# A two-layer attention, GLA and retention kernel: retention's gated branch goes by way of DRAM, attention's branch is projected last and by halves, attention's memory is handed on when it ends, background stages are spaced a little wider

## The chip, the cores and the metric

The kernel runs on one core of one Trainium2 chip. Its time is device microseconds from launch to end, the median of several runs; lower is better. The profile is one further execution of the same program, recorded instruction by instruction.

## The reference, cut to what matters

Two layers act on 1024 latent tokens `x` and 256 context tokens `xc`, each of 1024 columns. A layer normalizes and modulates its input, multiplies it by one wide matrix `w_in`, and splits the product into the inputs of three branches, three gates `z` (512 columns each) and three gates `g` (1024 columns each). The branches are neighbourhood attention (8 heads; each latent token sees a window of 8 x 16 latents and all the context), gated linear attention (GLA) and retention, both scanned in both directions with a state. All of them end in:

```python
def merge_branches(outs, z, g, w_branch, w_out):
    zs = jnp.split(z, N_BRANCH, axis=-1)
    gs = jnp.split(g, N_BRANCH, axis=-1)
    y = jax.nn.sigmoid(gs[0]) * ((outs[0] * jax.nn.silu(zs[0])) @ w_branch[0])
    for i in range(1, N_BRANCH):
        y = y + jax.nn.sigmoid(gs[i]) * ((outs[i] * jax.nn.silu(zs[i])) @ w_branch[i])
    return y @ w_out
```

The result is scaled by a gate from the modulation and added to the input. In layer 1 the context's own output is not needed, so queries, gates and merge run over 1024 tokens there and over 1280 in layer 0.

## The kernel before, in words

**Number format.** A dense product is three passes of TensorE: high part by high part, high by low, low by high (`mms`, line 376, is where every such matmul is recorded). So one unit of `fm` (128 output columns of `w_in` by 512 tokens) is 24 matmuls of 512 columns; the last token block of layer 0 has 256.

**Two programs interleaved by slots.** The instruction order is written out by a driver, `Drv`. `drv.gemm` is the dense stream: projections, then merge, layer by layer. Beside it run lanes and workers: `attention_lane` takes retention, GLA and neighbourhood attention one after another, and each spawns workers, one for a token chunk or for a unit of attention. In one `slot()` each worker and the dense stream are advanced twice, each lane once. The dense stream hands over after a quantum of `QUANT * drv.mult` = 3072 x `mult` matmul columns, or at the end of a unit if three quarters of that are reached (`end_unit`). So `mult` says how much dense work stands between two steps of the background. `RT_M`, `GL_M` and `NA_M1` are its values during retention, GLA (before and after attention's projections are done) and attention; it is 1.0 otherwise.

**Order of the dense stream.** Projections for retention, GLA, attention's v, then q and k; 12 groups of g gates, two units of 128 columns each and all token blocks (stored to DRAM after a tanh, line 1244); six groups of z gates in `Z_ORDER`, groups 0 and 1 for attention, 2 and 3 for GLA, 4 and 5 for retention. The evacuation of a z unit (`z_evac`, tanh at line 1259, product at 1260) loads the branch's output `o` back from DRAM (tile `ot`) and multiplies. For attention and GLA the product goes to DRAM (`b`, line 1273 and a deferred store); for retention it is split into a high and a low part in SBUF (lines 1267 to 1270). Groups 0 and 1 wait until attention has finished the first two, then all four of its head pairs (`na_out`); group 4 waits until the SBUF pool `E` exists.

**Attention** (`na`) has four pairs of heads; a pair has eight units of 128 queries, two more in layer 0 for the context. One unit is spawned every three slots. A unit loads q and its bias, computes scores, a softmax, transposes (`na_ptw`, `na_ptc`), copies them out of PSUM (`PT`, lines 992 and 995), multiplies by v (`na_o`, 1037) and copies the result (`oN`, 1040), which is stored when four units are together.

**After attention** the lane opens the pool `E` where attention's tiles were, if group 0 of z has begun (`want_E`). It then computes the modulation's gate (`mod_gate`: eight 512 KB pieces of `w_mod`, one a slot, matmuls `mod_ps` at line 210), and in layer 0 the next layer's shift and scale (`mod_ss`).

**Merge** takes the branches in the order 2, 1, 0 (retention, GLA, attention). Retention's operand is in SBUF already and a unit waits for its token block (`z_out`); the two others are loaded from DRAM and split by a worker, `load_b` (tiles `rb`, split at lines 1312 and 1313).

**Shared things.** Eight 128 x 512 buffers (`stg`) serve every evacuation and load named here: `st_g`, `st_z`, `ot`, `rb`, `gt`, `oN`. Nearly all loads and stores are issued in order by SP's queue. The `loader` lane brings half a weight group at a time: a load and a conversion (ScalarE cast at line 342, two GpSimd subtractions at line 345) need more than `LD_GAP` = 3 slots since the conversion before; a group that is needed earlier is converted on the spot (`need`).

Of the kernel before, what the change touches and what calls it, by code (L numbers as in the profile page):

```python
# [12 lines left out]
ALU = mybir.AluOpType  # L13
# [4 lines left out]
P = 128  # L18
# [12 lines left out]
NCOL = (24, 32, 32, 24)  # L31
LD_LAG, LD_GAP = 3, 3
RT_M = 1.25
GL_M = (1.1, 1.1, 1.0)
GL_N = 13
NA_M1 = 0.7
BR_ORDER = (2, 1, 0)
Z_ORDER = (2, 3, 0, 1, 4, 5)


def _next_f(c):
# [67 lines left out]
def hybrid_kernel(ctx: ExitStack, tc: tile.TileContext, A: dict, out: bass.AP):  # L109
    nc = tc.nc  # L110
    ctx.enter_context(tc.manual_schedule())
    pe, ve, sc, gp = nc.tensor, nc.vector, nc.scalar, nc.gpsimd
    drv = Drv()

    def dma(dst, src):
        nc.sync.dma_start(dst, src)
# [4 lines left out]
    def fv(ap):  # L121
        return ap.bitcast(F32)
# [26 lines left out]
    def stg(name, dt=F32):  # L149
        return pst.tile([P, 512], dt, tag="w2", name=name)  # L150
# [28 lines left out]
    def blocks(n):  # L179
        return [(t0, min(512, n - t0)) for t0 in range(0, n, 512)]  # L180
# [208 lines left out]
    def fm_unit(g, m, act, t0, nn, evac):  # L389
        ps = psg("fm")  # L390
        cs = m * P
        yield from mms(ps[:, :nn], nn,
                       ((lambda k: g.h(k, cs, P), lambda k: act.get(0, k, t0, nn)),
                        (lambda k: g.h(k, cs, P), lambda k: act.get(1, k, t0, nn)),
                        (lambda k: g.l(k, cs, P), lambda k: act.get(0, k, t0, nn))), g.kd)
        drv.evq_next.append(lambda: evac(m, t0, nn, ps[:, :nn]))
        if end_unit():
            yield
# [28 lines left out]
    L = []  # L427
    for layer in range(DEPTH):
# [6 lines left out]
        G = {}  # L435
# [12 lines left out]
        d = {"G": G, "nt": nt_out, "ntok": nt_out * P, "last": last}  # L448
# [197 lines left out]
    def gla(layer):  # L646
        d = L[layer]
        with tc.tile_pool(name=f"gla{layer}", bufs=2) as pl, tc.tile_pool(name=f"glac{layer}", bufs=1) as plc:
# [105 lines left out]

            drv.mult = GL_M[0]
            sc.preload_act_table_set("natural_log_exp_and_others")
# [130 lines left out]
    def na(layer):  # L887
        d = L[layer]
        ntok, last = d["ntok"], d["last"]
        with tc.tile_pool(name=f"na{layer}", bufs=2) as pn:  # L890
# [180 lines left out]
            for _ in range(4):  # L1071
                yield
            drv.mult = NA_M1
            for p in range(4):
# [42 lines left out]
    def projections(layer):  # L1117
        d = L[layer]
        while "h" not in d:
            yield  # L1120
        h = d["h"]
        G, nt, ntok, last = d["G"], d["nt"], d["ntok"], d["last"]
# [27 lines left out]
                    ga.done = True  # L1150
            gb.done = True

        def fm(g, ns, evac, by_block=False):
            need(g)
            units = [(m, t0, nn) for m in range(g.w // P) for t0, nn in blocks(ns[m])]
            if by_block:
                units.sort(key=lambda u: u[1])
            for m, t0, nn in units:
                yield from fm_unit(g, m, h, t0, nn, evac)
            g.done = True  # L1160

        yield from tm2(G["ret"][0], G["ret"][1], NT, spill_tm(d["ret"], 256, 256), spill_tm(d["ret"], 512, 256))
# [89 lines left out]
        def z_evac(zi):  # L1252
            def f(m, t0, nn, ps):
                r = zi * 256 + m * P
                br, ro = r // 512, r % 512
                ot = stg("ot")
                dma(ot[:, :nn], d["o"][br][ro:ro + P, t0:t0 + nn])
                st = stg("st_z")
                sc.activation(st[:, :nn], ps, AF.Tanh, scale=0.5)  # L1259
                ve.scalar_tensor_tensor(st[:, :nn], st[:, :nn], 1.0, ps, op0=ALU.add, op1=ALU.mult)  # L1260

                def w():
                    yield
                    yield
                    if br == 2:
                        bt = d["bact"][2]
                        ve.tensor_tensor(st[:, :nn], st[:, :nn], ot[:, :nn], op=ALU.mult)
                        hi, lo = bt.get(0, ro // P, t0, nn), bt.get(1, ro // P, t0, nn)
                        sc.copy(hi, st[:, :nn])
                        gp.tensor_tensor(lo, st[:, :nn], fv(hi), op=ALU.subtract)  # L1270
                        d["z_out"][t0] = d["z_out"].get(t0, 0) + 1
                    else:
                        gp.tensor_tensor(st[:, :nn], st[:, :nn], ot[:, :nn], op=ALU.mult)  # L1273
                        drv.defer(lambda: dma(d["b"][br][ro:ro + P, t0:t0 + nn], st[:, :nn]))
                drv.spawn(w())
            return f

        per_pair = 2 if last else 3
        d["z_out"] = {}
        for zi in Z_ORDER:  # L1280
            if zi < 2:
                while d.get("na_out", 0) < 2 * (zi + 1) * per_pair:
                    yield
            if zi == 0:
                d["want_E"] = True
            if zi == 4:
                while not d.get("E"):
                    yield
            yield from fm(G["z"][zi], [ntok] * 2, z_evac(zi), zi == 5)
        d["done"]["z"] = True  # L1290


    def merge(layer):
        d = L[layer]
        G, nt, ntok, last = d["G"], d["nt"], d["ntok"], d["last"]
        Ep = d["E"]
        y = Act(f"y{layer}", [U] * 5, KD, ntok, dt=F32, parts=1)
        bact = d["bact"]
        bact[1] = Act(f"bg{layer}", [U] * 5, 4, ntok)

        def load_b(br):
            pend = []
            for t0, nn in blocks(ntok) + [(None, 0)]:
                for k in range(4 if t0 is not None else 2):
                    if t0 is not None:
                        rb = stg("rb")
                        dma(rb[:, :nn], d["b"][br][k * P:(k + 1) * P, t0:t0 + nn])
                        pend.append((rb, k, t0, nn))
                    if len(pend) > 2 or t0 is None:
                        rb_, k_, u0, un = pend.pop(0)  # L1310
                        hi, lo = bact[br].get(0, k_, u0, un), bact[br].get(1, k_, u0, un)
                        sc.copy(hi, rb_[:, :un])
                        ve.tensor_tensor(lo, rb_[:, :un], fv(hi), op=ALU.subtract)
                    yield
                    yield

        def unit(g, br, bi, m, t0, nn):
            mt = m
# [32 lines left out]
            if end_unit():  # L1351
                yield

        w1 = drv.spawn(load_b(1))
        for bi, br in enumerate(BR_ORDER[:2]):
            if bi == 1:
                while not w1["done"]:
                    yield
                bact[0] = Act(f"bn{layer}", [Ep] * 5, 4, ntok)
                w1 = drv.spawn(load_b(0))  # L1360
            for mg in range(4):
                g = G["wb"][br][mg]
                need(g)
                for m in range(2):
                    for t0, nn in blocks(ntok):
                        while d["z_out"].get(t0, 0) < 4:
                            yield
                        yield from unit(g, br, bi, 2 * mg + m, t0, nn)
                g.done = True
        while not w1["done"]:  # L1370
# [2 lines left out]
        for t0, nn in blocks(ntok):  # L1373
            for m in range(8):
                g = G["wb"][0][m // 2]
# [28 lines left out]
        for gi in range(4):  # L1404
            g = G["wo"][gi]
# [8 lines left out]
    def attention_lane(layer):  # L1414
        d = L[layer]
        for key, fn in (("ret", retention), ("gla", gla), ("nqk", na)):
            while not d["done"].get(key):
                yield
            yield
            yield  # L1420
            yield from fn(layer)
        while not d.get("want_E"):
            yield
        es = d["es"] = ExitStack()
        ep = es.enter_context(tc.tile_pool(name=f"E{layer}", bufs=5))
        pgb = es.enter_context(tc.tile_pool(name=f"gb{layer}", bufs=1))
        E = (ep, "e")
        d["bact"] = {2: Act(f"br{layer}", [E] * 5, 4, d["ntok"])}
        d["E"] = E
        gate_sb = pgb.tile([98, 256], F32, tag="gate_sb", name="gate_sb")  # L1430
        d["gbc"] = [pgb.tile([P, D], F32, tag=f"gb{v}", name=f"gb{v}") for v in range(1 if d["last"] else 2)]
        with tc.tile_pool(name=f"modw{layer}", bufs=2) as pmw, tc.tile_pool(name=f"modp{layer}", bufs=1) as pm:
            yield from lane_join([drv.spawn(mod_gate(layer, pmw, gate_sb))])
            gd = dr.tile([2, D], F32, tag=f"gate_{layer}", name=f"gate_{layer}")
            for q in range(4):
                dma(gd[:, 256 * q:256 * q + 256], gate_sb[32 * q:32 * q + 2, :])
            yield
            for v, gb in enumerate(d["gbc"]):
                for q in range(2):
                    cs = slice(512 * q, 512 * q + 512)  # L1440
                    ob = stg("ob")
                    dma(ob, A["b_mod"][layer, 2048 + 512 * q:2560 + 512 * q].partition_broadcast(P))
                    dma(gb[:, cs], gd[v, cs].partition_broadcast(P))

                    def w(gb=gb, cs=cs, ob=ob):
                        for _ in range(4):
                            yield
                        gp.tensor_tensor(gb[:, cs], gb[:, cs], ob, op=ALU.add)
                    yield from lane_join([drv.spawn(w())])
            if not d["last"]:  # L1450
                yield from lane_join([drv.spawn(mod_ss(1, pm, pmw))])
        d["mod_done"] = True
# [201 lines left out]
```

## Time and profile before

| | us |
|---|---|
| median of 3 runs | 2956.39 (2952.46 to 2957.08) |
| profiled execution | 2953.91 |
| its span, first to last instruction | 2952.1 |
| TensorE matmul busy | 2828.3 (96%) |
| VectorE, ScalarE, GpSimd busy | 1499.4, 1102.1, 1078.2 |
| DMA | 418.69 MB, mean 142 GB/s |

Matmuls are pipelined, so a TensorE that is busy need not be at its peak. The idle time in front of an instruction matters only on the engine that bounds the stage. A group's line number can be that of a helper (376 for every dense matmul), so groups are told apart by tile names: `fm` is a projection by features, `tm` one by tokens, `mg` a merge product.

### The profile page before, as it was taken

Reading aid. Unit: us, or ns where it says so; the run is one execution under the profiler, and the core shown is the slowest. Engines: PE = TensorE matmul, PEld = TensorE weight load, DVE = VectorE, ACT = ScalarE, POOL = GpSimd, SP = SyncE. Lnnn points to the kernel's source line nnn. Section 1 sums busy time; section 2 is a strip of 40 time slices with the busy share of each in tenths; the row PEclk is TensorE's granted clock in tenths of the full one; section 3 lists DMA queues with packets and bytes.
Section 4 is the critical chain, followed back from the end, with each engine's and each line's share of the span. In section 5 each row is a group of like instructions: output and inputs, shape, how many; then the busy total and the mean of one; then the engine's idle time right before and its main releaser. Section 6 shows DMA issues by size and latency. Waiting matters only on the chain. (4 is left out here: it accounts for less than half of the span.)

```text
span 2952.1 us, 51923 instructions
## 1 busy us (share of the span) xinstructions
PE 2828.3 (96%) x19776; PEld 2433.6 (82%) x19776; DVE 1499.4 (51%) x3189; ACT 1102.1 (37%) x2569; POOL 1078.2 (37%) x1010
## 2 busy tenths in 40 slices
PE   7999999999999998899999999999999999879999
PEld 5999987788878887677899999987788788767889
DVE  5156567767514455424334346469766156562331
ACT  4133556554423434322113323456544244342110
POOL 4222125466411122043655332125665212204463
PEclk8999999999999999999999999999999999999999
DMA  6344433443244556467445354443433455645543
GB/s 239 107 142 130 139 105 111 115 133 104 92 144 135 170 151 189 125 199 233 136 126 149 104 166 119 132 121 109 145 111 111 148 160 182 181 125 164 183 129 108
DMA packets 390857, 418.69 MB, mean 142 GB/s; under 512 B 33788, under 2 KB 310284, under 8 KB 390608
## 3 DMA queue, kind: packets, MB, share of 16 engines
q1 hardware_dynamic: 353248, 361.59, 40.9%
q10 hardware_dynamic: 37360, 53.79, 5.2%
q8 instruction: 156, 2.56, 0.4%
q14 instruction: 93, 0.76, 0.1%
HBM read 302.72 MB, written 112.54 MB: 141 GB/s over the span
## 5 line engine op out<-in xcount | busy, mean ns | idle before, releaser
L376 PE MATMUL fm<-h,whi 128*128 128x512 f32 (+1 forms) x3936 | 922.6, 380 | 7.7 <-ACT st_g L1244 7.7
L345 POOL TENSOR_TENSOR wlo<-wraw,whi 128x512 fp32r<-128x512 f32 (+1 forms) x336 | 450.5, 1362 | 1000.4 <-ACT whi L342 892.0
L376 PEld LDWEIGHTS fm<-h,whi 128*128 128x128 f32 x3936 | 681.1, 190 | 157.8 <-issue 26.4
L376 PE MATMUL fm<-h,wlo 128*128 128x512 f32 (+1 forms) x1968 | 470.6, 374 | 0.0
L376 PEld LDWEIGHTS fm<-h,wlo 128*128 128x128 f32 x1968 | 339.8, 189 | 70.8 <-issue 8.7
L376 PE MATMUL tm<-whi,h 128*128 128x256 f32 (+1 forms) x2528 | 339.2, 284 | 2.0 <-ACT h L295 2.0
L376 PEld LDWEIGHTS tm<-whi,h 128*128 128x128 f32 x2528 | 318.2, 189 | 3.5 <-ACT h L295 2.7
L342 ACT CAST whi<-wraw 128x1024 fp32r<-128x1024 f32 (+1 forms) x168 | 175.8, 1048 | 268.4 <-PE tm L376 123.8
L376 PE MATMUL tm<-wlo,h 128*128 128x256 f32 (+1 forms) x1264 | 189.7, 286 | 0.0
L376 PEld LDWEIGHTS tm<-wlo,h 128*128 128x128 f32 x1264 | 166.6, 189 | 0.7 <-issue 0.2
L843 DVE TENSOR_TENSOR ek<-dd,kd 128x512 f32<-128x512 f32 x108 | 101.2, 937 | 93.4 <-ACT dd L833 93.2
L376 PE MATMUL tm<-whi,yy 128*128 128x256 f32 x1152 | 147.4, 280 | 0.0
L376 PEld LDWEIGHTS tm<-whi,yy 128*128 128x128 f32 x1152 | 140.7, 188 | 0.1
L1273 POOL TENSOR_TENSOR st_z<-st_z,ot 128x512 f32<-128x512 f32 (+1 forms) x40 | 48.2, 1209 | 253.1 <-DMA ot<-o 103.7
L798 POOL TENSOR_TENSOR dd<-Ac,ash 128x256 f32<-128x256 f32 x126 | 116.3, 923 | 51.5 <-ACT ash L785 31.0
L1260 DVE SCALAR_TENSOR_TENSOR st_z<-st_z,fm 128x512 f32<-128x512 f32 (+1 forms) x60 | 37.8, 633 | 174.4 <-ACT st_z L1259 172.5
L844 DVE SCALAR_TENSOR_TENSOR eq<-dd,g_col,qd 128x256 f32<-128x256 f32 x126 | 117.5, 933 | 13.1 <-ACT dd L833 13.0
L1244 ACT ACTIVATE st_g<-fm 128x512 f32<-128x512 f32 (+1 forms) x120 | 66.5, 557 | 144.0 <-PE fm L376 95.7
L1392 DVE TENSOR_TENSOR st_o<-tm,gb 128x256 f32<-128x256 f32 x72 | 30.5, 424 | 155.1 <-PE tm L376 152.0
L1334 DVE SCALAR_TENSOR_TENSOR gt<-gt,mg 128x512 f32<-128x512 f32 (+1 forms) x80 | 50.7, 634 | 112.5 <-PE mg L376 98.7
L833 ACT ACTIVATE dd<-dd 128x512 f32<-128x512 f32 x126 | 79.4, 635 | 75.3 <-POOL dd L799 73.1
L416 DVE COPY st_tm<-tm 128x256 f32<-128x256 f32 (+1 forms) x59 | 25.2, 428 | 161.5 <-PE tm L376 161.1
(1573 smaller groups left out, 4757.8 us busy)
## 6 DMA issues: line engine op xcount, KB each, us to landing
wraw<-in_w_in SPq DMA_DIRECT2D x104, 512.0 KB
wt<-in_w_mod SPq DMA_DIRECT2D x48, 512.0 KB
gd<-st_g ACTq DMA_DIRECT2D x96, 256.0 KB
gt<-gd SPq DMA_DIRECT2D x96, 256.0 KB
bt<-in_na_bm SPq DMA_DIRECT2D x32, 384.0 KB
ot<-o SPq DMA_DIRECT2D x48, 256.0 KB
wraw<-in_w_branch SPq DMA_DIRECT2D x24, 512.0 KB
v<-ret SPq DMA_DIRECT2D x38, 256.0 KB
```

The costliest lines, as they stand in the source:

```text
L342: sc.copy(hi[:, :, :w], raw[:, :, :w])
L345: gp.tensor_tensor(lo[:, ks, :w], raw[:, ks, :w], fv(hi[:, ks, :w]), op=ALU.subtract)
L376: pe.matmul(ps, a(k), b(k), start=i == 0, stop=i == tot - 1)
L798: gp.tensor_tensor(dv[:, :, Lh:], av[:, :, Lh:], rv, op=ALU.subtract)
L833: sc.activation(E_, E_, AF.Exp)
L843: ve.tensor_tensor(ek_, E_, kd_, op=ALU.mult)
L844: ve.scalar_tensor_tensor(eq[:, :, Lh:], ev[:, :, Lh:], rsc, qv[:, :, Lh:], op0=ALU.mult, op1=ALU.mult)
L1244: sc.activation(st[:, :nn], ps, AF.Tanh, scale=0.5)
L1260: ve.scalar_tensor_tensor(st[:, :nn], st[:, :nn], 1.0, ps, op0=ALU.add, op1=ALU.mult)
L1273: gp.tensor_tensor(st[:, :nn], st[:, :nn], ot[:, :nn], op=ALU.mult)
L1334: ve.scalar_tensor_tensor(gt[:, :nn], gt[:, :nn], 1.0, ps[:, :nn], op0=ALU.add, op1=ALU.mult)
L1392: ve.tensor_tensor(st[:, :256], ps, gbc[0 if t < LT else 1][:, 256 * gi:256 * gi + 256], op=ALU.mult)
```

## The change

Z groups 2 to 5 come first and 0 and 1 last; a wait can now be given for each half (128 columns) of a group, so each half of groups 0 and 1 waits for one more pair of attention's heads. All z products go to DRAM, retention's too. The pool `E` is opened as soon as attention's lane ends. `load_b` becomes a function of its own and also loads retention's branch, started by the lane after attention and once group 5's stores have had six slots; for that branch it takes one step of a worker for each piece, not two. Merge waits for it as a whole. `GL_M[2]` goes from 1.0 to 1.1, `NA_M1` from 0.7 to 0.8.

```diff
-GL_M = (1.1, 1.1, 1.0)
+GL_M = (1.1, 1.1, 1.1)
-NA_M1 = 0.7
+NA_M1 = 0.8
-Z_ORDER = (2, 3, 0, 1, 4, 5)
+Z_ORDER = (2, 3, 4, 5, 0, 1)
...
-        def fm(g, ns, evac, by_block=False):
+        def fm(g, ns, evac, wait=None):
             need(g)
-            units = [(m, t0, nn) for m in range(g.w // P) for t0, nn in blocks(ns[m])]
-            if by_block:
-                units.sort(key=lambda u: u[1])
-            for m, t0, nn in units:
-                yield from fm_unit(g, m, h, t0, nn, evac)
+            for m in range(g.w // P):
+                while wait is not None and not wait(m):
+                    yield
+                for t0, nn in blocks(ns[m]):
+                    yield from fm_unit(g, m, h, t0, nn, evac)
             g.done = True
...
-                    if br == 2:
-                        bt = d["bact"][2]
-                        ve.tensor_tensor(st[:, :nn], st[:, :nn], ot[:, :nn], op=ALU.mult)
-                        hi, lo = bt.get(0, ro // P, t0, nn), bt.get(1, ro // P, t0, nn)
-                        sc.copy(hi, st[:, :nn])
-                        gp.tensor_tensor(lo, st[:, :nn], fv(hi), op=ALU.subtract)
-                        d["z_out"][t0] = d["z_out"].get(t0, 0) + 1
-                    else:
-                        gp.tensor_tensor(st[:, :nn], st[:, :nn], ot[:, :nn], op=ALU.mult)
-                        drv.defer(lambda: dma(d["b"][br][ro:ro + P, t0:t0 + nn], st[:, :nn]))
+                    gp.tensor_tensor(st[:, :nn], st[:, :nn], ot[:, :nn], op=ALU.mult)
+                    drv.defer(lambda: dma(d["b"][br][ro:ro + P, t0:t0 + nn], st[:, :nn]))
...
         for zi in Z_ORDER:
+            wait = None
             if zi < 2:
-                while d.get("na_out", 0) < 2 * (zi + 1) * per_pair:
-                    yield
-            if zi == 0:
-                d["want_E"] = True
-            if zi == 4:
-                while not d.get("E"):
-                    yield
-            yield from fm(G["z"][zi], [ntok] * 2, z_evac(zi), zi == 5)
+                def wait(m, zi=zi):
+                    return d.get("na_out", 0) >= (2 * zi + m + 1) * per_pair
+            yield from fm(G["z"][zi], [ntok] * 2, z_evac(zi), wait)
+            if zi == 5:
+                def stored():
+                    for _ in range(12):
+                        yield
+                    d["want_b2"] = True
+                drv.spawn(stored())
...
+    def load_b(layer, br):
+        d = L[layer]
+        bact, ntok = d["bact"], d["ntok"]
...
                     yield
-                    yield
+                if br < 2:
+                    yield
...
-        w1 = drv.spawn(load_b(1))
+        while not d.get("b2") or not d["b2"]["done"]:
+            yield
+        w1 = drv.spawn(load_b(layer, 1))
...
-                        while d["z_out"].get(t0, 0) < 4:
-                            yield
...
-        while not d.get("want_E"):
-            yield
         es = d["es"] = ExitStack()
...
         d["E"] = E
+        while not d.get("want_b2"):
+            yield
+        d["b2"] = drv.spawn(load_b(layer, 2))
```

## Rows read from the trace of the kernel before

**Rows 1.** The page, part 1: an engine's busy time, share, instructions.
```profile
PE 2828.3 (96%) x19776; PEld 2433.6 (82%) x19776; DVE 1499.4 (51%) x3189; ACT 1102.1 (37%) x2569; POOL 1078.2 (37%) x1010
```
**Rows 2.** Waits of TensorE over the span: us in total, times, longest.
```profile
PE na_o L1037 <- DVE PT L992: 35.0, 19, 10.1
```
**Rows 3.** Sums by stage: busy us and instructions of each engine, clock, DMA, GB/s.
```profile
1158.60:1222.60 64.00, 44.76 (x363) 36.41 (x361) 44.31 (x151) 32.87 (x113) 7.07 (x6) 0.91 0.42 123
...
2347.00:2564.10 217.10, 217.10 (x1390) 179.92 (x1390) 126.50 (x350) 88.97 (x265) 45.56 (x35) 1.00 0.57 173
2564.10:2643.20 79.10, 53.23 (x442) 43.95 (x440) 52.37 (x175) 36.65 (x126) 6.54 (x5) 0.89 0.46 134
...
1325.00:1360.00 35.00, 35.00 (x217) 25.42 (x217) 18.05 (x37) 9.84 (x16) 9.27 (x8) 1.00 0.91 305
...
1232.00:1262.00 30.00, 30.00 (x184) 22.06 (x183) 5.28 (x10) 4.10 (x7) 6.02 (x6) 1.00 0.61 179
```
**Rows 4.** Chain of waits, layer 1: start us, length us, what.
```profile
2203.40 1.08 PE gla_lv L813 x32
...
2232.50 1.08 PE gla_lv L813 x32
...
2404.94 1.24 PE na_o L1037 x20
...
2435.72 1.25 PE na_o L1037 x20
...
2652.70 0.54 PE mod_ps L210 x8
...
2674.41 46.08 PE fm L376 x198
```
**Rows 5.** Sums by stage of line 1040 alone: ScalarE's busy us and instructions.
```profile
1158.60:1222.60 64.00, 2.93 (x11) 0.91 0.42 123
...
2564.10:2643.20 79.10, 2.93 (x11) 0.89 0.46 134
```
**Rows 6.** The page, part 5: count, busy us, mean ns, idle before.
```profile
L1273 POOL TENSOR_TENSOR st_z<-st_z,ot 128x512 f32<-128x512 f32 (+1 forms) x40 | 48.2, 1209 | 253.1 <-DMA ot<-o 103.7
...
L1260 DVE SCALAR_TENSOR_TENSOR st_z<-st_z,fm 128x512 f32<-128x512 f32 (+1 forms) x60 | 37.8, 633 | 174.4 <-ACT st_z L1259 172.5
```
**Rows 7.** Line 1244 in each layer: ns min/median/max, first to last start in us.
```profile
L1244 ACT ACTIVATE st_g<-fm x72: 364/592/619, 592.6 to 1039.6; 128x512 f32<-128x512 f32 x48, 128x256 f32<-128x256 f32 x24
...
L1244 ACT ACTIVATE st_g<-fm x48: 577/598/647, 2112.3 to 2464.3; 128x512 f32<-128x512 f32 x48
```
**Rows 8.** Timeline of SP's queue where attention's first loads are issued.
```profile
821.12 1.11 SPq L116 DMA_DIRECT2D k<-nkh  x2
...
2302.78 1.13 SPq L116 DMA_DIRECT2D k<-nkh  x2
```
**Rows 9.** Waits of TensorE from 593 to 840 and from 2105 to 2300.
```profile
PE gla_lv L813 <- DVE eq L845: 4.7, 4, 1.4
...
PE gla_lv L813 <- DVE eq L845: 3.6, 1, 3.6
```
**Rows 10.** Timeline of ScalarE, line 342, in layer 1's GLA stage.
```profile
2207.09 1.06 ACT L342 CAST whi<-wraw 128x1024 fp32r<-128x1024 f32 x1
...
2236.20 1.06 ACT L342 CAST whi<-wraw 128x1024 fp32r<-128x1024 f32 x1
```
**Rows 11.** Timeline of TensorE at three points; idle time before it in brackets.
```profile
1161.33 0.93 PE L1037 MATMUL na_o<-PT,vcx 128*64 128x128 f32 x8 [2.14 <-ACT PT L995]
...
2575.45 1.79 PE L1037 MATMUL na_o<-PT,vw 96*64 96x128 f32 x11 [10.06 <-DVE PT L992]
...
2647.56 0.75 PE L210 MATMUL mod_ps<-wt,csi 128*2 128x256 f32 x8 [2.72 <-DMA wt<-in_w_mod]
```
**Rows 12.** Timeline of ScalarE, layer 1, late in attention; idle before in brackets.
```profile
2573.61 0.60 ACT L1259 ACTIVATE st_z<-fm 128x512 f32<-128x512 f32 x1 [6.03 <-DMA b<-st_z]
```
**Rows 13.** DMA from 1325 to 1360, rate in 40 equal slices.
```profile
GB/s 389 293 173 384 375 377 187 288 349 358 222 367 373 310 355 411 386 377 215 276 361 358 225 332 376 321 345 342 324 373 392 231 37 194 251 73 164 306 369 377
```

More of the change, by code (lines that the diff above doesn't have):

```diff
@@ L1278, in projections @@
         per_pair = 2 if last else 3
-        d["z_out"] = {}
         for zi in Z_ORDER:
+            wait = None
             if zi < 2:
-                while d.get("na_out", 0) < 2 * (zi + 1) * per_pair:
-                    yield
-            if zi == 0:
-                d["want_E"] = True
-            if zi == 4:
-                while not d.get("E"):
-                    yield
-            yield from fm(G["z"][zi], [ntok] * 2, z_evac(zi), zi == 5)
-        d["done"]["z"] = True
+                def wait(m, zi=zi):
[7 more added lines that the diff above has]
+                drv.spawn(stored())
+        d["done"]["z"] = True
+    def load_b(layer, br):
+        d = L[layer]
+        bact, ntok = d["bact"], d["ntok"]
+        pend = []
+        for t0, nn in blocks(ntok) + [(None, 0)]:
+            for k in range(4 if t0 is not None else 2):
+                if t0 is not None:
+                    rb = stg("rb")
+                    dma(rb[:, :nn], d["b"][br][k * P:(k + 1) * P, t0:t0 + nn])
+                    pend.append((rb, k, t0, nn))
+                if len(pend) > 2 or t0 is None:
+                    rb_, k_, u0, un = pend.pop(0)
+                    hi, lo = bact[br].get(0, k_, u0, un), bact[br].get(1, k_, u0, un)
+                    sc.copy(hi, rb_[:, :un])
+                    ve.tensor_tensor(lo, rb_[:, :un], fv(hi), op=ALU.subtract)
+                yield
+                if br < 2:
+                    yield
     def merge(layer):
@@ L1299, in merge @@
         bact[1] = Act(f"bg{layer}", [U] * 5, 4, ntok)
[L1301 to L1313, printed above, removed]
-                    yield
-                    yield
         def unit(g, br, bi, m, t0, nn):
@@ L1359, in merge @@
                 bact[0] = Act(f"bn{layer}", [Ep] * 5, 4, ntok)
-                w1 = drv.spawn(load_b(0))
+                w1 = drv.spawn(load_b(layer, 0))
             for mg in range(4):
```

## The prediction

> **What bounds the kernel now.** I read the engine sums first, then the waits of TensorE, then the sums by stage, and last the chain of waits for the beat inside each stage. TensorE is busy for 96% of the span [rows 1], so a change pays only where TensorE stands idle or runs at half clock. Its longest waits in total are for VectorE's copy of the transposed probabilities, an instruction of neighbourhood attention [rows 2]. They lie in one place in each layer. Both stages called "starved" below begin when the projections have run out of work that is allowed and attention still has units to do: 1158.6 to 1222.6 in layer 0 and 2564.1 to 2643.2 in layer 1. There TensorE is busy for 44.76 of 64.0 us and 53.23 of 79.1 us, at a mean granted clock of 0.91 and 0.89, while the filled stage before (2347 to 2564.1) has it busy throughout at 1.00 [rows 3].
>
> The projections run dry because z0 waits for attention's first two pairs, z1 for all four, and z4 and z5 stand behind z1. After attention there are therefore z1, z4 and z5 still to do, with nothing beside them.
>
> **The beat.** Dense projection: 198 matmuls in 46.08 us, 0.2327 us for one of 512 columns. Filled attention: from 2404.94 to 2435.72 are three units, 10.26 us each. A unit is three slots, thus six quanta; at 0.7 a group of 24 matmuls is cut 5, 5, 5, 5, 4, so a unit brings 28.8 matmuls, 6.70 us. That leaves 3.56 us of TensorE for attention itself [rows 4]. Each starved stage shows 11 output copies [rows 5], a unit in 5.8 and 7.2 us: 11 x 3.56 = 39.2 us of real work, so 24.8 us are lost in layer 0 and 39.9 us in layer 1.
>
> **Part 1: z4 and z5 ahead of z0, and z0, z1 by halves.** Work is not changed, only its place. What it adds under attention, counted in 512-column matmuls: two groups (240 in layer 0, 192 in layer 1) and the first half of z1, which now needs only the third pair (60 and 48). Z4 and z5 bring their evacuations into the filled stage: a tanh, a VectorE and a GpSimd pass, one load and one store on SP's queue for each of 12 (8) units. In the filled stage VectorE is busy 126.5, ScalarE 89.0 and GpSimd 45.6 of 217.1 us [rows 3], so I cost the passes at nothing; without that cover VectorE's and GpSimd's are 0.63 and 1.21 us for a unit [rows 6], 15 us over eight of them. SP's two issues are weighed under part 5.
>
> **Part 2: GLA's multiplier 1.0 to 1.1** takes back part of this supply. It acts from the end of the attention projections to the end of GLA: 592.6 [rows 7] to 821.1 and 2112.3 to 2302.8 [rows 8]. Eight slots take 29.10 us there (2203.40 to 2232.50) [rows 4], 3.64 each, so these are 63 and 52 slots. The quantum grows from 3072 to 3379 columns, but matmuls are whole: in layer 1 two units of 24 are cut in seven pieces where there were eight, 12 to 13.71 a slot; in layer 0 a 512, 512, 256 triple is cut in nine where there were ten, 12 to 13.33. That is 84 and 89 matmuls more done beside GLA, which ends some 20 us later, with TensorE full in both cases. What it can win is the waits for VectorE in that stretch, 4.7 and 3.6 us [rows 9]; I take 2, bounds 0 and 8.3. What it can cost: the loader lane converts a half group at most every fourth slot; two ScalarE casts stand 29.1 us apart, with one between them [rows 10], exactly eight slots for a group. A group of layer 1 now lasts seven slots, so about every fourth group a half must be converted on the spot: two times a 1.05 us cast, 2 us; bounds 0 and 8 (every one of 52/7 groups).
>
> **Part 3: attention's multiplier 0.7 to 0.8.** With units of 512 columns five matmuls pass either threshold (2150 and 2458 columns), and the last four end the unit at 0.7 and at 0.8. Layer 1 is not changed at all. In layer 0 the 256-column units change the mean from 28.8 to 30 matmuls a unit: 28 units eat 34 more.
>
> **Part 4: the sum of the supply.** Layer 0: 240 + 60 - 84 - 34 = 182, at 30 a unit 6.1 of the 11 starved units are filled. Layer 1: 192 + 48 - 89 = 151, at 28.8 a unit 5.2 units. In shares of the lost time: layer 0 24.8 x 6.1/11 = 13.8 us. In layer 1 one wait of 10.06 us at the start of the starved stage is set aside: ScalarE stood 6.03 us for a store of a z product to land before it could reuse the buffer, and the probabilities queued behind it [rows 11, 12]. The rest gives (39.9 - 10.1) x 5.2/11 = 14.1 us.
>
> **Part 5: that hitch.** It comes when units shorten from 10.3 to 5.8 us and SP's queue, with its z loads and stores among attention's loads, falls behind. The same moment in layer 0 shows 2.14 us [rows 11]. One start with it and one without: I take half back, 5 us, bounds 10 saved and 10 more lost (a second one in layer 0).
>
> **Part 6: the way into the merge.** Retention's product now goes out to DRAM and comes back once attention has ended, because its tile lies in attention's memory. The store hides in the filled stage. The load can't: from attention's end to the first merge matmul stand only the last half of z1 and the gate's modulation matmuls. Bytes before that point: layer 0 twelve pieces 2.6 MB, eight modulation weights 4.2 MB, z1's loads and stores 1.3 MB, 8.1 MB; layer 1 (eight pieces, six weights by then) 6.3 MB. Cover: 60 x 0.2327 + 8 x 0.54 = 18.3 us, and 48 x 0.2327 + 6 x 0.54 = 14.4 us [rows 4]. TensorE's instructions stand in one written order, so a late modulation weight holds up z1 behind it: it waited 2.72 us for the first one already [rows 11]. SP's order is the same: each weight is issued behind one or two pieces, and a piece that has no free buffer holds the weights. The trace has no such stretch, so from both sides: at the 305 GB/s of 1325 to 1360, where weights, pieces and gates ran together and TensorE did not wait, 14.4 MB take 47.2 us, 14.5 over the cover; at that stretch's best slice, 411 GB/s [rows 13], 35.0, 2.3 over; at the 179 GB/s of 1232 to 1262 [rows 3] 80.4, 47.7 over. Nothing makes it a gain, as the loads are new. I take 10, near the first, whose mix of transfers it is.
> The row above shows 305 GB/s for transfers of 128 to 512 KB. The Trainium skill, "DMA: Bandwidth & Descriptors", section Bandwidth, asks for batches of 1 MiB or more and gives 341 GB/s at that size and 138 at 64 KB, which speaks against a round trip in 256 KB pieces. By 341 GB/s the 14.4 MB would cost an estimated 9.5 us over the cover, by 138 some 72; the trace's 305 lies near the first.
>
> **Sum.** 13.8 + 14.1 + 5 + 2 - 2 - 10 = 22.9 us less. The profiled execution took 2953.9 (its span is 2952.1), so 2931.0; the median of the runs is 2956.4, 2.5 us above it, and on that scale 2933.5.
>
> **Rivals.**
> *The way through DRAM decides (slower).* Place: the two entries into the merge. If the pieces and weights come at 179 GB/s because each waits for one of eight shared buffers, the entries cost 47.7 instead of 10: 22.9 - 37.7 = 14.8 us slower, 2971. It outweighs the rest from about 220 GB/s down (14.4 MB / 65.6 us, the cover plus the 32.9 us of gain). For it: the shared buffers already stop ScalarE [rows 12]. Against it: the mixed stretch at 305 with TensorE full [rows 3].
> *The widening eats the reorder (no change).* The supply goes into GLA, and both starts of starving show the 10 us wait: 13.8 + 14.1 - 10 - 14.5 - 4 = -0.6 us, thus 2957. For it: 173 of the 540 added matmuls go that way by count. Against: layer 0's start without it.
> *The fill reaches the end.* If attention needs less filler than counted, the lost time goes wholly: 64.7 + 2 - 2 - 10 = 54.7 us, 2902. Against it: the 11 units ask for 330 and 317 matmuls and get 182 and 151.
>
> **How the numbers follow.** Forecast (12 to 46 us less, 2910 to 2944) 0.72, full fill 0.05, no change 0.10, slower 0.13. The range, 2908 to 2957, takes in the no-change case and leaves out most of the full fill and of the slower case, some 0.17. A measurement of this kernel tells apart about 0.2%, 6 us. Faster than that 0.77, within it 0.10, slower 0.13.
>
> **What would show it.** Right: starved stages of some 30 us (five or six output copies without a projection between them) in each layer, eight z evacuations of layer 1 moved ahead of attention's end, only two after it; GLA ending 20 us later; merge entered 18 to 30 us earlier in total over both layers. Wrong: TensorE waiting more than 20 us for modulation weights or for retention's tile at the entries; a full-length starved stage; waits for the cast inside GLA.

## The result and the profile after

The changed kernel takes 2918.40 us in the median of 4 runs (2917.72 to 2921.78) where the kernel before took 2956.54: 38.1 us less, a ratio of 0.9876 with a 95% interval of 0.9859 to 0.9893. Forecast were 22.9 us less and 2933.5, in a range of 2908 to 2957. The profiled execution took 2921.78, the longest of its four, against 2953.91 before, so of the 38 us the two traces show 32.

On the page TensorE is busy for 7.7 us less than before [rows 1], in a span 32.1 us shorter. So 24.4 of the 32.1 us that went are idle time:

```profile
PE 2820.6 (97%) x19776; PEld 2426.7 (83%) x19776; DVE 1517.4 (52%) x3189; ACT 1099.5 (38%) x2569; POOL 1077.7 (37%) x1010
```

The waits of TensorE after (total us, times, longest). The wait for the transposed probabilities, 35.0 before [rows 2], has gone to 19.0; a wait for a weight cast of 9.8 is new:

```profile
PE mod_ps L210 <- DMA wt<-in_w_mod: 21.4, 19, 6.6
PE na_o L1037 <- DVE PT L992: 19.0, 10, 5.4
...
PE fm L376 <- ACT whi L342: 9.8, 1, 9.8
```

Sums by stage after (columns as in [rows 3]): attention without filler in layer 0, the entry into the merge, the merge; then the same for layer 1, where the first row is a stretch with filler that stops twice.

```profile
1236.20:1266.50 30.30, 20.26 (x169) 16.30 (x167) 18.51 (x62) 13.61 (x49) 1.95 (x2) 0.91 0.27 85
1266.50:1289.80 23.30, 21.33 (x122) 13.99 (x121) 8.82 (x14) 8.59 (x17) 1.29 (x1) 0.82 0.84 269
1289.80:1474.80 185.00, 182.04 (x1018) 143.79 (x1015) 80.54 (x135) 36.03 (x58) 94.39 (x75) 1.00 0.65 210
...
2577.20:2638.10 60.90, 53.92 (x345) 44.48 (x345) 36.79 (x102) 23.43 (x71) 15.66 (x13) 0.94 0.59 177
2638.10:2670.00 31.90, 24.16 (x214) 19.83 (x212) 23.13 (x76) 15.17 (x54) 1.27 (x1) 0.95 0.31 93
2670.00:2688.60 18.60, 15.72 (x81) 10.03 (x81) 5.96 (x9) 5.61 (x10) 1.67 (x1) 0.91 0.82 273
```

The 64.0 and 79.1 us without filler [rows 3] are 30.3 and 31.9 now. Line 1040, the copy of a unit's output, counts the attention units that end in them, five each where there were 11 [rows 5] (in layer 0 one copy more starts 0.1 us behind the row's edge, before and after):

```profile
1236.20:1266.50 30.30, 1.33 (x5) 0.91 0.27 85
2638.10:2670.00 31.90, 1.33 (x5) 0.95 0.31 93
```

GLA ends later, as the first load of attention shows. Line 1244 and SP's queue, the answers to [rows 7] and [rows 8]: the stretch from the first gate to attention's first load has grown from 228.5 to 243.5 us in layer 0 and from 190.5 to 212.3 in layer 1.

```profile
L1244 ACT ACTIVATE st_g<-fm x72: 377/583/643, 592.5 to 1013.4; 128x512 f32<-128x512 f32 x48, 128x256 f32<-128x256 f32 x24
...
L1244 ACT ACTIVATE st_g<-fm x48: 579/598/643, 2091.4 to 2439.3; 128x512 f32<-128x512 f32 x48
```
```profile
836.03 1.11 SPq L116 DMA_DIRECT2D k<-nkh  x2
...
2303.71 1.11 SPq L116 DMA_DIRECT2D k<-nkh  x2
```

The entry into the merge of layer 0 in TensorE's timeline (start, length, idle before in brackets): a wait of 1.97 us for the first modulation weight, and behind it twelve matmuls take 4.63 us that take 3.05 a little later. Four matmuls in front of the wait are slow too: 2.08 us, against 1.20 for the four in the last line. The mean granted clock of this stage is 0.82 (row above); the last section shows where it fell.

```profile
1266.46 2.08 PE L376 MATMUL fm<-h,whi 128*128 128x512 f32 x4
1270.50 1.03 PE L210 MATMUL mod_ps<-wt,csi 128*2 128x256 f32 x8 [1.97 <-DMA wt<-in_w_mod]
1271.46 4.63 PE L376 MATMUL fm<-h,whi 128*128 128x512 f32 x12
...
1280.09 3.05 PE L376 MATMUL fm<-h,whi 128*128 128x512 f32 x12
...
1289.79 1.20 PE L376 MATMUL mg<-br,whi 128*128 128x512 f32 x4
```

Before the change TensorE waited for the first modulation weight at the same point, when attention had ended: 2.72 us in layer 1 [rows 11], and in layer 0:

```profile
1226.61 0.61 PE L210 MATMUL mod_ps<-wt,csi 128*2 128x256 f32 x8 [1.48 <-DMA wt<-in_w_mod]
```

### The profile page after: what moved, and what is told of

Its sections match the earlier page's. It is cut to its first block, busy times and chain, and to the rows that moved or that the text cites. A ratio compares the mean times of both kernels' runs of the same rounds, so it can differ in the third digit from the quotient of the medians.

```text
span 2920.0 us, 52004 instructions
## 1 busy us (share of the span) xinstructions
PE 2820.6 (97%) x19776; PEld 2426.7 (83%) x19776; DVE 1517.4 (52%) x3189; ACT 1099.5 (38%) x2569; POOL 1077.7 (37%) x1010
## 5 line engine op out<-in xcount | busy, mean ns | idle before, releaser
L376 PEld LDWEIGHTS fm<-h,whi 128*128 128x128 f32 x3936 | 679.6, 190 | 157.2 <-issue 24.4
L1265 POOL TENSOR_TENSOR st_z<-st_z,ot 128x512 f32<-128x512 f32 (+1 forms) x60 | 73.8, 1237 | 260.7 <-DMA ot<-o 108.7
L799 POOL TENSOR_TENSOR dd<-ash,Ac 128x256 f32<-128x256 f32 x126 | 106.4, 844 | 0.0
L813 PEld LDWEIGHTS gla_lv<-eq,ek 128*64 128x64 f32 x2016 | 67.5, 139 | 42.0 <-issue 24.3
```

The costliest lines, as they stand in the source:

```text
L376: pe.matmul(ps, a(k), b(k), start=i == 0, stop=i == tot - 1)
L799: gp.tensor_tensor(dv[:, :, :Lh], rv, av[:, :, :Lh], op=ALU.subtract)
L813: pe.matmul(pl_[bk, x, h, :], ek_[:, h, bk], eq_[:, h, bk if lv else bq], start=True, stop=True)
```

## The experiments

Each ran beside the kernel before on its own chip, which takes 2952 to 2957 us from one chip to the next; I compare ratios. One per mille is 3 us. An interval reaches some 5 us to either side, so a difference between two of these kernels has to be about 7 us to be clear of the noise.

| kernel | ratio | 95% interval |
|---|---|---|
| the change | 0.9876 | 0.9859 to 0.9893 |
| multipliers alone, on the kernel before | 1.0076 | 1.0060 to 1.0091 |
| order, way and pool alone | 0.9860 | 0.9846 to 0.9875 |
| change, NA_M1 0.7 | 0.9864 | 0.9849 to 0.9879 |
| change, NA_M1 0.6 | 0.9846 | 0.9830 to 0.9863 |
| change, gate after the load | 0.9851 | 0.9836 to 0.9866 |
| change, stores a slot later | 0.9872 | 0.9855 to 0.9888 |
| change, whole groups | 0.9933 | 0.9916 to 0.9949 |
| NA_M1 0.6 and gate after the load | 0.9817 | 0.9803 to 0.9832 |
| the same with GL_M[2] 1.0 | 0.9812 | 0.9797 to 0.9826 |

**The multipliers alone.**
```diff
-GL_M = (1.1, 1.1, 1.0)
+GL_M = (1.1, 1.1, 1.1)
-NA_M1 = 0.7
+NA_M1 = 0.8
```


> The kernel before with the two multipliers alone changed (GL_M[2] 1.1, NA_M1 0.8), z order, retention's way and the pool as before. Theory A, supply: what counts is how much dense work is left when attention runs. The wider steps eat 118 matmuls in layer 0 and 89 in layer 1, so 3.9 and 3.1 more units run without filler, at some 2.6 us lost for each: 18 us slower, less about 4 us of waits saved in GLA: 2966 to 2975. Theory B, spacing: the wider steps help by themselves, because GLA's and attention's chains get more time for a step: 3 to 10 us faster, 2946 to 2953.

2977.32 us, 1.0076: slower, as supply says, by 22 us, a little more than its range. The stages without filler grow from 64.0 and 79.1 to 88.2 and 73.3 us, in layer 1 with a second stand of 20 us at 2538 outside the row:
```profile
1142.10:1230.30 88.20, 61.82 (x496) 51.10 (x495) 57.86 (x199) 40.24 (x144) 7.50 (x6) 0.90 0.37 107
2594.20:2667.50 73.30, 54.81 (x450) 45.79 (x448) 55.52 (x179) 36.61 (x126) 6.79 (x5) 0.91 0.45 131
```
Spacing as a gain in itself falls: without the reorder the wider steps are a loss.

**The rest alone** (the changed kernel).
```diff
-GL_M = (1.1, 1.1, 1.1)
+GL_M = (1.1, 1.1, 1.0)
-NA_M1 = 0.8
+NA_M1 = 0.7
```


> The changed kernel with both multipliers back (GL_M[2] 1.0, NA_M1 0.7): order, halves, DRAM way and pool alone. Theory A, supply: 118 and 89 matmuls more are there for attention, 3 to 4 units fewer without filler in each layer, 10 to 18 us, less 4 us of waits that come back in GLA: 2904 to 2912 (the changed kernel has 2918). Theory B, spacing: 5 to 15 us slower than the changed kernel, 2924 to 2933.

2913.83 us, 0.9860: the whole gain is here. Order, DRAM way and pool were not run one by one. It is 5 us better than the change by the ratios, on supply's side but short of its 2904 to 2912, and the intervals overlap. Its stages without filler are down to 4.5 and 21.8 us:
```profile
1260.00:1264.50 4.50, 2.79 (x21) 1.69 (x21) 2.44 (x4) 1.20 (x4) 3.27 (x3) 0.86 0.34 109
2637.60:2659.40 21.80, 16.55 (x138) 13.66 (x135) 16.17 (x43) 9.14 (x30) 5.25 (x4) 0.84 0.39 119
```

**NA_M1 0.7 alone.**
```diff
-NA_M1 = 0.8
+NA_M1 = 0.7
```


> The changed kernel with NA_M1 back at 0.7 alone. By the count of whole matmuls layer 1 is cut exactly as with 0.8 (pieces of 5, 5, 5, 5, 4), and layer 0 takes 28.8 instead of 30 matmuls for a unit: 34 to 40 matmuls more are left, a bit over one unit without filler less there: 2 to 4 us faster, 2914 to 2916, layer 1 the same within 1 us. Spacing: slower by 1 to 3 us.

2914.72 us, 0.9864, 3.5 us less, as counted, but within the noise. The trace is the better witness: layer 0's stage shrinks from 30.3 to 19.0 us, layer 1's stays at 31.9, since its pieces are the same.
```profile
1241.40:1260.40 19.00, 13.03 (x121) 10.32 (x121) 11.75 (x42) 8.13 (x29) 1.27 (x2) 0.97 0.23 74
2629.10:2661.00 31.90, 24.24 (x214) 19.95 (x212) 23.16 (x76) 15.18 (x54) 1.27 (x1) 0.95 0.32 93
```
This kernel and the last one differ in `GL_M[2]` alone, 1.1 here and 1.0 there. There the stages are 14.5 and 10.1 us shorter, yet the time is only about 1 us less, far within the noise. A part of it was lost again behind the stage of layer 0: TensorE waited 5.74 us for the first modulation weight there, 1.43 us here, and the way into the merge took 27.2 us there (from 1264.4 on, mean clock 0.77) and 20.9 here (from 1260.4 on, 0.95).

**NA_M1 0.6.**
```diff
-NA_M1 = 0.8
+NA_M1 = 0.6
```


> The changed kernel with NA_M1 at 0.6: a unit of 24 matmuls is cut in six pieces of four, so a unit of attention takes 24 matmuls of filler instead of 30 (layer 0) and 28.8 (layer 1). Theory A, supply: filler lasts for 5 to 8 units more, the stages without filler (30 us in layer 0, 46 in layer 1) all but vanish, 15 to 27 us less: 2891 to 2903. Theory B, spacing: at 9.1 us a unit instead of 10.3 the probabilities come late in the filled stage, TensorE waits there, 0 to 15 us more: 2918 to 2933.

2908.34 us, 0.9846, 9 us less than the change: right in direction, about half of what supply asked, though the intervals just overlap. The stage without filler is gone in layer 0 (the last 41 us of attention have TensorE busy throughout) and is 6.9 us in layer 1:
```profile
1200.00:1241.30 41.30, 41.30 (x283) 34.62 (x282) 22.97 (x57) 15.49 (x47) 11.96 (x10) 1.00 0.35 112
...
2641.40:2648.30 6.90, 4.54 (x50) 3.45 (x50) 5.48 (x10) 1.41 (x4) 3.66 (x4) 1.00 0.38 124
```
So 9.1 us for a unit is long enough for attention's chain; but a stage that vanishes gives back only what TensorE lost in it, not its length.

**Whole groups instead of halves.**
```diff
-                    return d.get("na_out", 0) >= (2 * zi + m + 1) * per_pair
+                    return d.get("na_out", 0) >= 2 * (zi + 1) * per_pair
```


> The changed kernel with the waits of z0 and z1 for whole groups again: z1 as a whole waits for all four pairs, everything else as changed. By the supply theory the halves bring 60 and 48 matmuls under attention, two units with filler in layer 0 and 1.7 in layer 1 at 2.6 to 3 us each, so without them 9 to 11 us more: 2927 to 2930; and the entry into the merge, now with four or six units of z1 to cover the modulation's weights and retention's pieces, gives 0 to 5 us of it back: 2922 to 2930. If the halves are worth nothing because the entry is only as long as its transfers, 2918.

2933.97 us, 0.9933: 17 us slower than the change, more than any case had it. The stages are 44.7 and 49.1 us:
```profile
1214.70:1259.40 44.70, 30.64 (x246) 24.87 (x243) 29.56 (x94) 21.47 (x73) 7.41 (x6) 0.90 0.35 109
2621.20:2670.30 49.10, 37.04 (x327) 30.43 (x325) 38.39 (x123) 25.26 (x85) 6.30 (x5) 0.97 0.44 134
```
So 108 matmuls, 25.1 us at 0.2327, are worth 17 us under attention by the ratios and 12 between the two profiled executions (2933.97 and 2921.78): half to two thirds of their time is free there. The prediction had 32.9 us for 333 matmuls, 77.5 us, a share of 0.42. With the noise (17 us, 7 to either side) that is not excluded.

**The gate after retention's load.**
```diff
+            yield from lane_join([d["b2"]])
             yield from lane_join([drv.spawn(mod_gate(layer, pmw, gate_sb))])
```


> The changed kernel with the modulation's gate started only when retention's branch is loaded: its eight 512 KB weights no longer stand among the twelve (eight) pieces. The entries into the merge take 23.3 and 18.6 us in the changed kernel. If they are held by bytes and by the wait for weights (my prediction's part 6), they shrink to about 15 and 13 us and the modulation matmuls come later under the merge: 3 to 8 us less in all, 2910 to 2915. Rival: the entry is slow because TensorE comes out of the stage without filler at a low clock (0.82 and 0.91 there), whatever the weights do: within 2 us of 2918.

2910.90 us, 0.9851, 7 us less, at the edge of the noise; on top of `NA_M1` 0.6 (below) it takes off 9. The entries are 14.0 and 11.1 us, just the 60 and 48 matmuls of z1's last half, at a clock of 1.00:
```profile
1265.50:1279.50 14.00, 14.00 (x73) 11.89 (x73) 8.36 (x14) 8.30 (x16) 1.53 (x2) 1.00 0.70 206
2661.70:2672.80 11.10, 11.10 (x48) 9.04 (x49) 6.69 (x9) 5.12 (x10) 1.68 (x1) 1.00 0.69 213
```
Retention's pieces alone cost TensorE nothing in the entries. What was lost hung on the modulation weight in front of z1's matmuls and on the low clock. How much of the clock was the weight's doing is shown in layer 1 only, where the clock fell at the end of that wait (last section). In layer 0 it had fallen 3.8 us before the wait, in the stage without filler, so the rival that blamed that stage is not ruled out there: the stage is as long here (29.4 us without a dense matmul, 30.3 in the change) and the clock did not fall at its end, but that is one profile.

**The store one slot later.**
```diff
-                    drv.defer(lambda: dma(d["b"][br][ro:ro + P, t0:t0 + nn], st[:, :nn]))
+                    drv.defer(lambda: drv.defer(lambda: dma(d["b"][br][ro:ro + P, t0:t0 + nn], st[:, :nn])))
```


> The changed kernel with the store of each z product issued one slot later. In layer 1 TensorE stands at the same unit of attention before and after the change (10.1 and 5.4 us), ScalarE waiting 6.0 us for such a store to land. Theory Q: SP's queue stands for the product (12 waits, 53 us, longest 14.5, in layer 1's attention) and all of attention's loads stand behind; a slot later the product is there, the stand at that unit goes, 3 to 8 us less: 2910 to 2915. Theory B: the eight shared buffers are what is short, and a store a slot later keeps them longer: 0 to 10 us more, 2918 to 2928.

2917.05 us, 0.9872: no difference clear of the noise. Theory B's loss is not seen, and a gain as small as the low end of theory Q could not be told. In layer 1's attention SP stands 53.3 us for z products in the change and 30.2 here,
```profile
SPq L116 <- POOL st_z L1265: 53.3, 12, 14.5
```
```profile
SPq L116 <- PE na_sc L929: 50.1, 17, 6.7
SPq L116 <- POOL st_z L1265: 30.2, 11, 6.8
```
but it now waits longer for attention's own tiles: 50.1 against 34.2. At the same unit ScalarE still waits 4.1 us for a store, 1.9 less than in the change, and TensorE stands 3.50 us (from 2576.71 to 2580.21), also 1.9 less. So the time of the store bears on that stand. What makes up the rest is left open.

**Two together, and three.** The gate after the load with NA_M1 0.6; and with GL_M[2] 1.0 besides.

> As e5 but GL_M[2] stays at 1.1: NA_M1 0.6 and the gate after retention's load. If the two gains add: 2918 - 9 - 7 = 2902. If they overlap: 2907. Against e5 it tells what GLA's multiplier is worth when attention has filler enough: by supply 0 to 5 us in favour of e5.

> The changed kernel with three settings that should each help by the supply theory: NA_M1 0.6, the modulation's gate after retention's load, GL_M[2] back to 1.0. The first two took 9 and 7 us off alone. The third gives 89 and 84 matmuls back to attention, which by then has enough, so it should only trade: the 9.8 us wait for the cast where attention of layer 1 begins goes (it is 4.8 with 1.0), some 4 us of waits in GLA come back. Supply: 2897 to 2903. If the gains overlap (the entry into the merge is slow only after a stage without filler), 2905 to 2910.

2901.01 us, 0.9817, and 2899.37 us, 0.9812. The two gains add within the noise, and the second is the fastest version measured: 17 and 19 us under the change, outside its interval. GLA's multiplier makes no difference that can be told (1.5 us). It trades: with 1.0 TensorE waits 5.3 us where attention of layer 1 begins, with 1.1 it waits 10.2, and GLA's waits go the other way (line 845: 13.2 us with 1.0, 11.3 with 1.1). Waits of TensorE from 2280 to 2345, first with 1.0, then with 1.1:
```profile
PE fm L376 <- ACT st_g L1244: 5.3, 1, 5.3
```
```profile
PE fm L376 <- ACT whi L342: 10.2, 1, 10.2
```

## Why the prediction was right, and where it was off

**Part 1 and part 4, the supply: right in mechanism, and in size over both layers.** The stages without filler came out at 30.3 and 31.9 us with five units each (forecast: some 30 us, five or six). The multipliers alone and the whole groups moved the way of the supply, clear of the noise; `NA_M1` 0.7 did in its trace. The lost time of layer 0, 24.8 us, was set too low. It charged all 11 units at the 3.56 us of a latent unit, but three of the 11 are context units; the row of [rows 11] at 1161.33 is one, with only eight matmuls where a latent unit has twenty. Such a unit takes some 1.4 us of TensorE in the trace of before (0.48 scores, 0.35 transposes, 0.58 output, at 956 to 963). 8 x 3.56 + 3 x 1.4 = 32.7 leaves 31.3 us lost. After the change 30.3 - 4 x 3.56 - 1.4 = 14.7 are lost there, 16.6 less (forecast 13.8). In layer 1 it is 39.9 before; after, 31.9 - 5 x 3.56 = 14.1, and 10.4 more in the 60.9 us ahead (125 dense matmuls and six units, 50.5 us of work): 15.4 less (forecast 14.1 and the 5 of the hitch).

**The term that was mis-sized most is part 6, the way into the merge: 10 us, and it cost nothing.** Set against the traces, the terms come out like this (us less; a term's loss of time is negative):

| term | forecast | traces |
|---|---|---|
| parts 4 and 5: lost time at the end of attention | 32.9 | 32.0 |
| part 2: waits for VectorE in GLA | 2 | 3.0 |
| part 2: the cast | -2 | -5.4 |
| part 6: the entries into the merge | -10 | 0.1 |
| not in the sum: wait at the start of attention, layer 0 | | 4.1 |
| not in the sum: the two merges, without work moved into them | | -2.2 |
| sum | 22.9 | 31.6 |

From the first gate to the end of the merge layer 0 takes 882.3 us, 19.6 less than before; from there to the end of its own merge layer 1 takes 1350.9, 12.4 less: 32.0 together. So what the forecast had too little of is nearly all part 6; the other differences cancel, by luck. Another 6 us lie between medians and profiled executions. The merge was entered 42 us earlier in total, not 18 to 30 (697.3 against 727.4 us from the first gate, and in layer 1 1213.8 against 1226.0 from the end of layer 0's merge).

The wait at the start of layer 0's attention is the 5.2 us that TensorE stands from GLA's end to the stage without filler before (busy for 332.33 of the 337.50 us from 821.10 to 1158.60), against 1.1 after (399.14 of 400.20, from 836.00 to 1236.20).

**Part 2, GLA's multiplier.** GLA takes 15 and 22 us longer (forecast 20). Of the waits of [rows 9] layer 0's go from 4.7 to 0.9, layer 1's line 845 from 3.6 to 4.4, together 3 us, where I took 2. The loader did not fall behind inside GLA. It did where attention begins: the 9.8 us wait for a cast, which was 4.4 for another cause before:
```profile
PE fm L376 <- ACT st_g L1244: 4.4, 1, 4.4
```
It appears with 1.1 in all profiles and in none with 1.0. The term was 2 us, at the wrong place, and measures some 5. The supply that the multiplier takes, 84 and 89 matmuls, did show in the length of the stages (14.5 and 10.1 us between the two kernels that differ in it alone), but hardly in the time.

**Part 3** was right: layer 1 does not change between 0.7 and 0.8.

**Part 5, the hitch: wrong.** I took it for a start of starving. It comes at the same unit of attention in the change, with filler still running, 5.42 us with ScalarE again waiting for a store of a z product. TensorE, then ScalarE, after:
```profile
2582.66 1.79 PE L1037 MATMUL na_o<-PT,vw 96*64 96x128 f32 x11 [5.42 <-DVE PT L992]
```
```profile
2580.82 0.60 ACT L1259 ACTIVATE st_z<-fm 128x512 f32<-128x512 f32 x1 [6.04 <-DMA b<-st_z]
```
The half that I took back (10.06 to 5.42) is there, for another reason than mine: the unit takes 15.9 us from its output to the next in both traces (2559.51 to 2575.45 and 2566.71 to 2582.66), and what fills part of it now is 20 dense matmuls more, 4.65 us.

**Part 6, the way into the merge: the step that failed.** The entries take 23.3 and 18.6 us. Without modulation weights they take 14.0 and 11.1; six and four groups of modulation matmuls of 0.54 us stand in them (3.2 and 2.2). That leaves 6.1 and 5.3 lost, 11.4 us. That looks like the 10 forecast, but the forecast was a loss added to what the place lost already. Between attention and the merge before the change
```profile
1222.60:1320.00 97.40, 95.92 (x554) 72.72 (x554) 21.26 (x32) 18.79 (x32) 34.06 (x28) 0.99 0.60 184
...
2643.20:2720.50 77.30, 74.58 (x354) 55.70 (x354) 14.31 (x22) 14.96 (x23) 27.57 (x21) 0.98 0.54 171
```
there are 360 and 288 dense matmuls of 512 columns (83.8 and 67.0 us) and 15 and eight modulation groups (8.1 and 4.3), which leaves 5.5 and 6.0 lost, 11.5 us. So the way into the merge lost no more than before, where 10 us more were forecast. What is lost there is of the same kind in both, as far as rows show it: the wait for the first weight (1.48 and 2.72 us, then 1.97 and 2.88) and work at the low clock. The prediction priced the new transfers by their bytes and did not ask what the old entry lost; its own row of the 2.72 us wait showed a part. The rate was 269 and 273 GB/s. The page of the Trainium skill named in the prediction, "DMA: Bandwidth & Descriptors", section Bandwidth, asks for batches of 1 MiB or more; here the 256 KB pieces cost TensorE nothing in the entries once the weights stood behind them. No run changed the size of a piece.

The sum also left out the merge of layer 0, 10.5 us longer than before (185.0 against 174.5). Modulation matmuls that stood beside z1, z4 and z5 now stand in it. Line 210 alone in the merge, after and then before:
```profile
1289.80:1474.80 185.00, 11.09 (x148) 1.91 (x144) 1.00 0.65 210
```
```profile
1320.00:1494.50 174.50, 5.52 (x72) 0.96 (x72) 1.00 0.55 176
```
That is 5.6 us of work moved, not added. TensorE waits 2.8 us more there for VectorE; some 2 us are unexplained. Layer 1's merge takes 137.1 us with 2.5 us of such moved work, 137.3 before without.

**The rivals.** The way through DRAM did not decide, the widening did not eat the reorder, the fill did not reach the end, though `NA_M1` 0.6 showed that it can in layer 0.

## What to carry to other kernels

Where a bound engine starves in one stage, count the work that may run there, and count it in whole instructions: of two settings of a multiplier one layer may see no difference at all. Work moved under a starved stage is worth the engine's idle time, so price each kind of background unit by itself before multiplying. When a stage has been emptied of filler, look at what stands first in the bound engine's queue behind it: a late operand there costs its wait and, in layer 1 here, the clock as well. And before pricing a new loss at some place, count what that place loses already: only the difference is the change's.

## What the runs showed of the hardware

TensorE's granted clock around the entries of the changed kernel, layer 0 (four rows), then layer 1; 0.50 is the lower of its two levels, 1.2 of 2.4 GHz:
```profile
1260.00:1264.70 4.70, 2.25 (x19) 1.51 (x17) 2.09 (x8) 1.93 (x7) 0.00 (x0) 1.00 0.15 56
1264.70:1268.50 3.80, 3.36 (x12) 2.15 (x12) 0.39 (x1) 1.53 (x4) 0.00 (x0) 0.50 0.25 25
1268.50:1270.50 2.00, 0.03 (x2) 0.03 (x1) 0.30 (x1) 0.00 (x0) 0.00 (x0) 0.50 0.94 359
1270.50:1274.90 4.40, 4.40 (x16) 2.87 (x17) 1.35 (x2) 1.85 (x3) 0.00 (x0) 0.50 1.05 394
...
2670.00:2674.40 4.40, 1.62 (x7) 1.01 (x6) 0.69 (x1) 0.89 (x2) 0.00 (x0) 1.00 0.71 201
2674.40:2677.80 3.40, 3.30 (x14) 1.99 (x15) 1.36 (x2) 1.24 (x2) 0.00 (x0) 0.50 1.04 411
```
In layer 0 the clock fell at 1264.7, in the stage without filler, after 4.7 us in which TensorE was busy for 2.25; the wait for the weight came 3.8 us later. It rose at 1274.9, after 4.4 us of work without a gap. Over the 23.3 us of the entry the mean of 0.82 makes 8.4 us at the lower level; 2.0 of them are the wait, so 6.4 us of work ran at half speed and 3.2 us were lost, besides the wait of 1.97. In layer 1 the clock was 1.00 through the wait of 2.88 us and 0.50 for 3.4 us from its end on: 1.7 us lost, less than the wait.

With the gate after the load the same end of the stage in layer 0 ran at 1.00 (first row), with TensorE busy for 2.61 of 5.5 us. With the store one slot later, where the weight was waited for from 1267.9 to 1270.1, the clock fell before the wait, was up through it, and fell again after it (the other two rows):
```profile
1260.00:1265.50 5.50, 2.61 (x24) 1.63 (x21) 1.93 (x8) 2.58 (x9) 0.00 (x0) 1.00 0.23 69
```
```profile
1264.30:1267.70 3.40, 3.13 (x12) 2.15 (x12) 0.15 (x1) 1.38 (x4) 0.00 (x0) 0.50 0.28 19
...
1271.10:1274.50 3.40, 3.40 (x10) 2.65 (x9) 1.34 (x2) 1.73 (x3) 0.00 (x0) 0.50 1.01 383
```
So in layer 0 one profile of each kernel does not settle what the weight's wait costs by the clock. Nor does the mean clock of the span follow the gain: it was 0.984 to 0.990 in the runs of the kernel before, 0.986 to 0.987 in those of the change, and 0.988 to 0.994 in those of the fastest version.
